# Storing the last of eight results through a SyncE register instead of a DMA

## Chip, cores, metric

One core of a Trainium2 chip. The metric is the device time of one execution in microseconds; a version is timed as the median of several executions. Times of this kernel agree within about 0.3 us from run to run.

## The reference

```python
# a, b: float32 [8, 2176, 2176]
prod = np.matmul(a, b)
return np.diagonal(prod, axis1=1, axis2=2).sum(axis=-1)     # 8 float32
```

Only the traces are wanted: each batch is the sum over the elements of `a` transposed times `b`. 303 MB of input give 32 bytes of output.

## The kernel before

All of `a` and `b` but the first 128 rows of `a` (1.1 MB, from SyncE's queue) is loaded from GpSimd's queue, which casts float32 to bfloat16 on the way. TensorE transposes `a`, ScalarE and VectorE copy the transposes from PSUM to SBUF ("evacuate"), VectorE multiplies and reduces (`multiply_reduce`), and in the last batch TensorE takes a part of the products into `trace_ps`. These parts matter here:

```python
def load(src, start, m):
    t = stage.tile([P, ROWS, N], bf16, tag="stage")
    rows = src[start:start + P * m, :].rearrange("(p r) k -> p r k", r=m)
    issued = nc.gpsimd.dma_start(out=t[:, 0:m, :], in_=rows)
    return t, issued
# ... the last row of b, in three pieces, also from GpSimd:
b_t = stage.tile([P, ROWS, N], bf16, tag="stage")
row = b_t[:, 0, :]
for g0, g1 in LAST_PIECES:                       # [(0, 2), (2, 3), (3, 5)]
    lo, hi = g0 * WIDE, min(g1 * WIDE, N)
    nc.gpsimd.dma_start(out=row[:, lo:hi], in_=b[bi, start:start + P, lo:hi])
# ...
multiply_reduce(tiles[f32], trace_ps, late_acc[:, len(late):len(late) + 1])

total = psum_small.tile([1, BATCH], f32, tag="total")
nc.tensor.matmul(
    total[:, 0:BATCH - 1], tiles["ones"], tiles["sums"][:, 0:BATCH - 1],
    start=True, stop=True,
)
parts = [tiles["sums"][:, BATCH - 1:BATCH]] + [late_acc[:, n:n + 1] for n in range(len(late) + 1)]
for n, part in enumerate(parts):
    nc.tensor.matmul(
        total[:, BATCH - 1:BATCH], tiles["ones"], part,
        start=(n == 0), stop=(n == len(parts) - 1),
    )
nc.vector.tensor_copy(out=tiles["result"][:1, :BATCH], in_=total)
nc.sync.dma_start(out=out.rearrange("(a b) -> a b", a=1), in_=tiles["result"][:1, :BATCH])
```

Behind this the build adds a closing sequence: each engine executes an instruction called DRAIN, SyncE checks the semaphores of all queues and engines one after the other (the "closing checks"), each engine signals to GpSimd at a barrier, GpSimd passes when all have signalled and releases them, and after a second round of that barrier the program ends. A transfer "lands" where the trace records the last semaphore update that it makes.

Of the kernel before, what the change touches and what calls it, by code (L numbers as in the profile page):

```python
# [20 lines left out]
def kernel(  # L21
# [6 lines left out]
    nc = tc.nc  # L28
    P = 128
    BATCH, N, N2 = a.shape  # L30
# [5 lines left out]
    f32 = mybir.dt.float32  # L36
# [9 lines left out]
    const = ctx.enter_context(tc.tile_pool(name="const", bufs=1))  # L46
# [5 lines left out]
    psum_small = ctx.enter_context(tc.tile_pool(name="psum_small", bufs=1, space=bass.MemoryType.PSUM))  # L52
# [18 lines left out]
    tiles = {}  # L71

    def constants():
        identity32 = const.tile([P, P], f32, tag="identity32")
        make_identity(nc, identity32)
        identity16 = const.tile([P, P], bf16, tag="identity16")
        make_identity(nc, identity16)
        ones = const.tile([P, 1], f32, tag="ones")
        nc.vector.memset(ones, 1.0)
        sums = const.tile([P, BATCH], f32, tag="sums")  # L80
        late = const.tile([P, 4], f32, tag="late")
        result = const.tile([P, BATCH], f32, tag="result")
        tiles.update(ones=ones, sums=sums, late=late, result=result)
        tiles[f32], tiles[bf16] = identity32, identity16

    evacs = 0
# [9 lines left out]
    def multiply_reduce(x, y, acc):  # L96
        scratch = scratch_pool.tile([P, N], bf16, tag="scratch")
        out = scratch[:, :math.prod(x.shape[1:])]
        if len(x.shape) == 3:
            out = out.rearrange("q (a b) -> q a b", b=x.shape[2])  # L100
        elif len(x.shape) == 4:
            out = out.rearrange("q (a b c) -> q a b c", b=x.shape[2], c=x.shape[3])
        nc.vector.tensor_tensor_reduce(  # L103
            out=out, in0=x, in1=y, scale=1.0, scalar=0.0,
            op0=MUL, op1=ADD, accum_out=acc,
        )
# [79 lines left out]
    late = []  # L186
    ahead = None
    for bi in range(BATCH):
# [6 lines left out]
        for start, m in order:  # L195
            if not tiles:
                a_t = load_first(a[bi], start)
                ahead, issued = load(a[bi], *order[1])
                with tc.issue_after(issued.ins):
                    constants()  # L200
            elif ahead is not None:
                a_t, ahead = ahead, None
            else:
                a_t, _ = load(a[bi], start, m)
            last_transpose = transpose_group(at, a_t, start, m, b_groups)
# [9 lines left out]
        for gi, (start, m) in enumerate(b_groups):  # L215
# [33 lines left out]
            out=tiles["sums"][:, bi:bi + 1], in_=acc[:, :cols], axis=mybir.AxisListType.X  # L249
# [4 lines left out]
    with tc.issue_after(last_transpose.ins):  # L254
        for n, (x, y) in enumerate(pe_work):
            nc.tensor.matmul(  # L256
                trace_ps, x, y, start=(n == 0), stop=(n == len(pe_work) - 1),
            )
    late_acc = tiles["late"]
    for n, (x, y) in enumerate(late):  # L260
        multiply_reduce(x, y, late_acc[:, n:n + 1])
    multiply_reduce(tiles[f32], trace_ps, late_acc[:, len(late):len(late) + 1])

    total = psum_small.tile([1, BATCH], f32, tag="total")
    nc.tensor.matmul(
        total[:, 0:BATCH - 1], tiles["ones"], tiles["sums"][:, 0:BATCH - 1],
        start=True, stop=True,
    )
    parts = [tiles["sums"][:, BATCH - 1:BATCH]] + [late_acc[:, n:n + 1] for n in range(len(late) + 1)]
    for n, part in enumerate(parts):  # L270
        nc.tensor.matmul(  # L271
            total[:, BATCH - 1:BATCH], tiles["ones"], part,
            start=(n == 0), stop=(n == len(parts) - 1),
        )
    nc.vector.tensor_copy(out=tiles["result"][:1, :BATCH], in_=total)
    nc.sync.dma_start(
        out=out.rearrange("(a b) -> a b", a=1),
        in_=tiles["result"][:1, :BATCH],
    )


# [28 lines left out]
```

## Time and profile before

| | before |
|---|---|
| time, median of the first 3 runs | 711.72 us (711.46 to 711.79) |
| span of the profiled execution | 709.78 us |
| last landing of `b` | 705.60 us |
| copy of the eight results ends on VectorE | 707.07 us |
| their store lands | 708.16 us |
| SyncE signals at the closing barrier | 708.31 us |
| GpSimd's closing drain ends | 709.03 us |
| GpSimd passes the barrier | 709.07 us |

Times inside a span count from its start; the last rows are read from the trace's records of semaphores and sequencers. The busy shares, the end of the timeline and the closing records are shown in the prediction below.

### The profile page before, as it was taken

The numbers are of one execution on the slowest core, as the hardware profiler recorded it, in microseconds if no ns is written. First come the engines' busy times: TensorE is split into PE (matmuls) and PEld (weight loads), VectorE is DVE, ScalarE is ACT, GpSimd is POOL, SyncE is SP. The second block draws the span as 40 slices with busy tenths as digits, with TensorE's granted clock in tenths as the row PEclk, the third lists the DMA queues.
The fourth block names the chain that finished last, engine by engine and source line by source line (L and its number), as shares of the span: only waits on it lengthen the run. The fifth ranks groups of instructions, "written<-read, shape, count | busy, mean of one in ns | idle before, by whom it ended". The sixth has DMA issues, their size and how long they took to land.

```text
span 709.8 us, 3800 instructions
## 1 busy us (share of the span) xinstructions
PE 233.3 (33%) x1406; PEld 221.8 (31%) x1406; DVE 408.9 (58%) x449; ACT 201.6 (28%) x210; POOL 45.2 (6%) x91
## 2 busy tenths in 40 slices
PE   2660025600345003540036400374003630036356
PEld 1660025600344003540036400374003630036355
DVE  0327972279812898219972199621996319963146
ACT  2651015600256002550035500354003630036300
POOL 2000000000000000000000000000000000000010
PEclk9866556755588555885556755666556875567755
DMA  9999999999999999999999999999999999999997
GB/s 220 220 220 219 206 219 219 220 218 206 221 219 218 218 210 218 220 218 214 213 219 219 218 213 214 220 218 216 213 217 219 218 216 212 218 218 216 219 210 139
DMA packets 12116, 152.32 MB, mean 215 GB/s; under 512 B 1346, under 2 KB 1602, under 8 KB 3778
## 3 DMA queue, kind: packets, MB, share of 16 engines
q0 software_dynamic: 11952, 150.97, 100.1%
q1 hardware_dynamic: 146, 1.11, 0.4%
q8 instruction: 11, 0.18, 0.1%
q14 instruction: 7, 0.06, 0.0%
HBM read 303.04 MB, written 0.00 MB: 427 GB/s over the span
## 4 chain that ended last, share of the span: by engine, by line
DMA 52%; issue 43%; POOL 3%; PE 2%; DVE 1%; another core or an unknown queue 0%; POOLq 0%; DVEq 0%
DMA t<-in_a_dram 42%; DMA t<-in_b_dram 6%; DMA b_t<-in_b_dram 3%; POOL t L57 2%; PE ps L136 1%; PE trace_ps L256 1%; DVE scratch L103 0%; DVE at L91 0%; POOL b_t L222 0%; POOLq L57 0%; PE ps L157 0%; POOL identity masks.py:199 0%; PE total L271 0%; POOL identity masks.py:197 0%
## 5 line engine op out<-in xcount | busy, mean ns | idle before, releaser
L103 DVE CUSTOM_DVE_ANT_1 scratch<-at,t 128x2048 bf16<-128x2048 bf16 (+1 forms) x156 | 310.5, 1990 | 85.5 <-DMA t<-in_b_dram 78.9
L136 PE MATMUL ps<-identity,t 128*128 128x128 f32 x1071 | 204.2, 372 | 460.3 <-DMA t<-in_a_dram 297.7
L136 PEld LDWEIGHTS ps<-identity,t 128*128 128x128 f32 x1071 | 193.7, 218 | 468.3 <-issue 302.8
L93 ACT COPY at<-ps 128x1024 bf16<-128x1024 bf16 x208 | 199.2, 1016 | 471.2 <-PE ps L136 471.1
L91 DVE COPY at<-ps 128x1024 bf16<-128x1024 bf16 (+2 forms) x104 | 92.8, 902 | 205.8 <-PE ps L136 198.9
L57 POOL DMA_DIRECT2D t<-in_a_dram x39 | 20.8, 535 | 329.5 <-DVE acc L103 230.2
L57 POOL DMA_DIRECT2D t<-in_b_dram x41 | 21.7, 530 | 304.2 <-PE ps L157 286.5
L256 PEld LDWEIGHTS <-at 128*128 128x128 bf16 x153 | 17.4, 124 | 12.0 <-issue 12.0
L256 PE MATMUL trace_ps<-t,at 128*128 128x128 bf16 x144 | 17.3, 294 | 10.2 <-DMA t<-in_b_dram 10.2
L157 PE MATMUL ps<-identity,t 128*128 128x128 bf16 x170 | 17.0, 224 | 2.2 <-DVE at L91 2.2
L157 PEld LDWEIGHTS <-t 128*128 128x128 bf16 x170 | 13.4, 102 | 3.8 <-issue 3.4
L103 DVE DVE_READ_ACCUMULATOR2_ANT acc<- 128x1 f32 x163 | 13.3, 82 | 0.0
L68 DVE CAST t<-words 128x1088 bf16<-128x1088 f32 x1 | 0.7, 726 | 4.9 <-DMA words<-in_a_dram 4.9
L103 DVE CUSTOM_DVE_ANT_0 scratch<-at,t 128x128 bf16<-128x128 bf16 x7 | 2.0, 291 | 0.2
L67 ACT CAST t<-words 128x1088 bf16<-128x1088 f32 x1 | 1.1, 1098 | 3.7 <-DMA words<-in_a_dram 3.7
L222 POOL DMA_DIRECT2D b_t<-in_b_dram x3 | 1.6, 539 | 3.6 <-PE trace_ps L256 3.6
L256 PE MATMUL trace_ps<-b_t,at 128*128 128x128 bf16 x9 | 1.5, 287 | 0.5 <-DMA b_t<-in_b_dram 0.4
L103 DVE CUSTOM_DVE_ANT_1 scratch<-at,b_t 128x256 bf16<-128x256 bf16 (+1 forms) x3 | 1.5, 510 | 0.2 <-DMA b_t<-in_b_dram 0.2
L248 DVE TENSOR_REDUCE sums<-acc 128x1 f32<-128x22 f32 (+1 forms) x8 | 1.4, 174 | 0.3
L67 ACT ACT_TABLE_LOAD x1 | 1.3, 1283 | 0.7 <-PEq L294 0.7
L271 PE MATMUL total<-late,ones 128*1 128x1 f32 x8 | 0.5, 163 | 0.3 <-DVE late L103 0.3
masks.py:199 POOL TENSOR_SCALAR_AFFINE_SELECT identity<-identity 128x128 f32<-128x128 f32 (+1 forms) x2 | 0.6, 308 | 0.0
(14 smaller groups left out, 2.4 us busy)
## 6 DMA issues: line engine op xcount, KB each, us to landing
t<-in_a_dram POOLq DMA_DIRECT2D x32, 2176.0 KB, 42.3
t<-in_b_dram POOLq DMA_DIRECT2D x31, 2176.0 KB, 47.2
t<-in_b_dram POOLq DMA_DIRECT2D x9, 544.0 KB, 39.5
t<-in_a_dram POOLq DMA_DIRECT2D x7, 544.0 KB, 35.0
words<-in_a_dram SPq DMA_DIRECT2D x1, 1088.0 KB, 5.0
t<-in_b_dram POOLq DMA_DIRECT2D x1, 1088.0 KB, 41.7
b_t<-in_b_dram POOLq DMA_DIRECT2D x1, 256.0 KB, 23.0
b_t<-in_b_dram POOLq DMA_DIRECT2D x1, 160.0 KB, 23.4
```

Of the source, the lines that this page charges most:

```text
L57: issued = nc.gpsimd.dma_start(out=t[:, 0:m, :], in_=rows)
L67: nc.scalar.copy(out=t[:, 0, :half], in_=plain[:, :half])
L68: nc.vector.tensor_copy(out=t[:, 0, half:], in_=plain[:, half:])
L91: nc.vector.tensor_copy(out=dst, in_=src)
L93: nc.scalar.copy(out=dst, in_=src)
L103: nc.vector.tensor_tensor_reduce(out=out, in0=x, in1=y, scale=1.0, scalar=0.0, op0=MUL, op1=ADD, accum_out=acc,)
L136: nc.tensor.transpose(ps[:, n * m + r, :], words[:, r, c0:c0 + step * (P - 1) + 1:step], tiles[f32],)
L157: last_transpose = nc.tensor.transpose(ps16[:, n, r, :], a_t[:, r, c0:c0 + P], tiles[bf16],)
L222: nc.gpsimd.dma_start(out=row[:, lo:hi], in_=b[bi, start:start + P, lo:hi])
L248: nc.vector.reduce_sum(out=tiles["sums"][:, bi:bi + 1], in_=acc[:, :cols], axis=mybir.AxisListType.X)
L256: nc.tensor.matmul(trace_ps, x, y, start=(n == 0), stop=(n == len(pe_work) - 1),)
L271: nc.tensor.matmul(total[:, BATCH - 1:BATCH], tiles["ones"], part, start=(n == 0), stop=(n == len(parts) - 1),)
```

## The change

Its intent: the store of the result at the very end is a DMA, which took 1.06 us from issue to landing. Seven of the eight results are known 74 us earlier, so they are stored then. For the eighth, SyncE loads the one word from SBUF into a register and stores it straight to memory, without a DMA.

```diff
+        last_sum = const.tile([P, 2], f32, tag="last_sum")
 ...
+    out_words = out.rearrange("(a b) -> a b", a=1)
+    result, last_sum = tiles["result"], tiles["last_sum"]
     total = psum_small.tile([1, BATCH], f32, tag="total")
     nc.tensor.matmul(
         total[:, 0:BATCH - 1], tiles["ones"], tiles["sums"][:, 0:BATCH - 1],
         start=True, stop=True,
     )
-    parts = [tiles["sums"][:, BATCH - 1:BATCH]] + [...]
+    nc.vector.tensor_copy(out=result[:1, :BATCH - 1], in_=total[:, :BATCH - 1])
+    nc.sync.dma_start(out=out_words[:, :BATCH - 1], in_=result[:1, :BATCH - 1])
+    final = psum_small.tile([1, 1], f32, tag="final")
+    parts = [tiles["sums"][:, BATCH - 1:BATCH]]
+    parts += [late_acc[:, n:n + 1] for n in range(len(late) + 1)]
     for n, part in enumerate(parts):
         nc.tensor.matmul(
-            total[:, BATCH - 1:BATCH], tiles["ones"], part,
-            start=(n == 0), stop=(n == len(parts) - 1),
+            final, tiles["ones"], part, start=(n == 0), stop=(n == len(parts) - 1),
         )
-    nc.vector.tensor_copy(out=tiles["result"][:1, :BATCH], in_=total)
-    nc.sync.dma_start(out=..., in_=tiles["result"][:1, :BATCH])
+    nc.vector.tensor_copy(out=last_sum[:1, 0:1], in_=final)
+    words = last_sum.bitcast(mybir.dt.int32)
+    last_word = out_words.bitcast(mybir.dt.int32)[:, BATCH - 1:BATCH]
+    word = nc.sync.alloc_register("word")
+    nc.sync.load(word, words[:1, 0:1])
+    nc.sync.store(last_word, word)
```

More of the change, by code (lines that the diff above doesn't have):

```diff
@@ L82, in constants @@
         result = const.tile([P, BATCH], f32, tag="result")
-        tiles.update(ones=ones, sums=sums, late=late, result=result)
+        last_sum = const.tile([P, 2], f32, tag="last_sum")
+        tiles.update(ones=ones, sums=sums, late=late, result=result, last_sum=last_sum)
         tiles[f32], tiles[bf16] = identity32, identity16
@@ L268 @@
     )
-    parts = [tiles["sums"][:, BATCH - 1:BATCH]] + [late_acc[:, n:n + 1] for n in range(len(late) + 1)]
+    nc.vector.tensor_copy(out=result[:1, :BATCH - 1], in_=total[:, :BATCH - 1])
[3 more added lines that the diff above has]
+    parts += [late_acc[:, n:n + 1] for n in range(len(late) + 1)]
     for n, part in enumerate(parts):
         nc.tensor.matmul(
-            total[:, BATCH - 1:BATCH], tiles["ones"], part,
-            start=(n == 0), stop=(n == len(parts) - 1),
-        )
-    nc.vector.tensor_copy(out=tiles["result"][:1, :BATCH], in_=total)
-    nc.sync.dma_start(
-        out=out.rearrange("(a b) -> a b", a=1),
-        in_=tiles["result"][:1, :BATCH],
-    )
+            final, tiles["ones"], part, start=(n == 0), stop=(n == len(parts) - 1),
+        )
+    nc.vector.tensor_copy(out=last_sum[:1, 0:1], in_=final)
[4 more added lines that the diff above has]
+    nc.sync.store(last_word, word)
 _INS = ['a', 'b']
```

## The prediction

> **What bounds the kernel now.** I began with the page: busy shares, slices, DMA queues.
>
> ```profile
> PE 233.3 (33%) x1406; PEld 221.8 (31%) x1406; DVE 408.9 (58%) x449; ACT 201.6 (28%) x210; POOL 45.2 (6%) x91
> DMA  9999999999999999999999999999999999999997
> q0 software_dynamic: 11952, 150.97, 100.1%
> ```
>
> No engine is over 58% busy, while the DMA engines are at nine tenths or more in 39 of 40 slices, and the queue fed by GpSimd alone takes 100.1% of the 16 engines' span. The kernel is a stream of `a` and `b` into SBUF; everything up to the last landing is set by that stream. The change touches nothing in it on purpose, so it can only act after the last landing, or by disturbing the stream. Next, the timeline of the last microseconds (start, duration, what).
>
> ```profile
> 705.64 0.50 PE L256 MATMUL trace_ps<-b_t,at 128*128 128x128 bf16 x3 [0.41 <-DMA b_t<-in_b_dram]
> 706.34 0.29 DVE L103 CUSTOM_DVE_ANT_0 scratch<-identity,trace_ps 128x128 bf16<-128x128 f32 x1 [0.18 <-PE total L271]
> 706.69 0.19 PE L271 MATMUL total<-late,ones 128*1 128x1 f32 x2 [0.28 <-DVE late L103]
> 706.91 0.15 DVE L275 COPY result<-total 1x8 f32<-1x8 f32 x1 [0.28 <-PE total L271]
> 707.10 0.32 SPq L276 DMA_DIRECT2D out_dram<-result  x1
> ```
>
> The last piece of `b` lands at 705.60 us, and 1.47 us of dependent work follow until the copy of the result ends at 707.07. SyncE issues the store at 707.10; the two semaphore updates of that DMA come at 707.54 and 708.16 us. The store costs 1.06 us from issue to landing. The span is 709.8 us, so 1.6 us come after even that. The chain of waits ends at the copy and says nothing of them; the sequencers' records of the line that closes the program do (count, then min/median/max ns, then first and last start).
>
> ```profile
> L305 SPq EVENT_SEMAPHORE  x8: 17/28/28, 707.5 to 709.7; - x8
> L305 POOLq EVENT_SEMAPHORE  x4: 17/17/17, 709.1 to 709.7; - x4
> L305 POOLq DRAIN  x3: 45/95/27027, 682.0 to 709.5; - x3
> L305 SPq DRAIN  x3: 7/7/7, 708.2 to 709.3; - x3
> ...
> SPq L305 <- PEq L305: 1.4, 2, 0.9
> SPq L305 <- DMA out_dram<-result: 0.4, 1, 0.4
> ```
>
> This is what decides the case. GpSimd begins its closing drain at 682.0 us, right behind its last load, and the drain lasts 27.027 us: it ends at 709.03. GpSimd then gathers the other engines at a barrier (709.07) and the program ends 0.71 us later. SyncE, which had the store to wait for (0.4 us of wait, the last line), reached that barrier at 708.31 us by the trace's semaphore record, and then waited 0.9 us. The view blames PE's sequencer for the 0.9, but PE had drained by 706.93: the one still missing was GpSimd. So the store of the result is *not* the last thing to arrive; it has 709.03 - 708.31 = 0.72 us of slack, if GpSimd's drain does not itself depend on that store.
>
> **What the Trainium skill says.** (1) "DMA: Bandwidth & Descriptors", section "Anatomy of one DMA", gives a DMA a fixed cost of about 2.0 us, most of it the write receipt. That is its fit for the GpSimd path; the trace here has 1.06 us for the 32-byte store from SyncE, so the prize is about half of what the page suggests. (2) The same page, "Latency and other measured facts", puts the floor of a `tensor_load` at about 600 ns. (3) "Runtime: NRT & Kernel Launch", section "Instruction fetch mechanics", puts a register load at about 200 ns a register in bulk and a store to HBM at about 73 ns, because a store is posted and a load is a round trip. The kernel before has neither, so its trace can't confirm (2) and (3). (4) The first page, "How a descriptor splits into AXI transactions": a descriptor that doesn't start on 256 B fetches from the boundary below. I use it for a side effect below.
>
> **The change part by part.** The order in which the built instructions stand shows where the scheduler put them.
>
> *Seven results early.* Their matmul already stands early (0.20 us at 632.74 us in the trace). Behind it DVE gets one copy of 1x7, about 0.15 us like the 1x8 copy. DVE is idle then: it ends an evacuation at 632.37 and has nothing until 633.65. Copy from about 632.96 to 633.12: hidden, with 0.5 us to spare. The 28-byte store runs from about 633.2 beside the stream: one or two small packets among 12116; the 32-byte one took 7 ns of one DMA engine. Cost 0.0 us, and its landing is 70 us before the end.
>
> *The arithmetic tail.* The same five final matmul pairs, now to a bank of their own, then a 1x1 copy in place of 1x8. 0.0 us; the copy again ends near 707.07.
>
> *The store.* Removed: the issue (0.32 us, 707.10 to 707.42) and its flight to 708.16. Added on SyncE, one behind the other: a load of the word from SBUF, a load of the output's 64-bit address from memory (two registers; the build adds it, the diff doesn't show it), one 64-bit addition, the store. Estimate from (2) and (3): 0.6 + 0.6 + 0.05 (sequencer steps at the end of this trace take 0.01 to 0.05) + 0.07 = 1.32 us. So the store is done at 707.10 + 1.32 = 708.42 us.
>
> *The closing waits.* Before, SyncE ran five of its six semaphore checks while the DMA flew: they start 0.06 us apart from 707.47 to 707.72, and only the sixth waited. Now all seven stand behind the store: a branch of 0.05, 7 x 0.062 = 0.43, and two drains of 0.055 each, 0.11. That is 0.59 us which used to lie beside the flight. SyncE reaches the barrier at 708.42 + 0.59 = 709.01 us, against 708.31 before: 0.70 us *later*.
>
> *The sum.* GpSimd ends its drain at 709.03 in either kernel. 709.01 against 709.03 is a tie: change 0.0 us if the loads cost their floor. The effect is one-sided: faster loads gain nothing because GpSimd is there, slower ones are paid in full. The skill's "about 1.3 us" for the load sequence of the launch (same runtime page) is an address read from HBM like the second load; with that in place of 0.6, SyncE arrives at 709.71 and the end moves by 0.68 us. I weigh the floor somewhat more than the other and take +0.2 us: 711.72 + 0.18 = 711.9 us.
>
> **The rivals.** *A: the store's latency was the end, and the register path saves it.* For it: SyncE waited on the store's landing, and GpSimd's drain ended 0.87 us after the landing, so it might be a consequence of it. Against it: GpSimd waits on no semaphore of that store, it was draining for 25 us before the store was issued, and its own last load landed at 705.60, 3.43 us before; a fixed overhead after that is as natural. If A holds and both loads take 0.2 us a register (three registers, 0.6 us in all), SyncE arrives at 708.3, as before: the gain is at most the drain's share, 0.7 us, so 711.0. I give a gain of over 0.3 us 12%.
>
> *B: two round trips cost much more than the floor.* Nothing in the trace speaks against it, since no register load is in it. At 1.3 us each the sum is 2.72, SyncE arrives at 710.41, and the time is 1.4 us longer: 713.1. I give over 0.9 us 10%.
>
> *C: the stream is disturbed.* The new tile of two words moves every large tile by 32 bytes in the build: the staging tiles started on multiples of 256 bytes and no longer do. 16 engines work all the time, so a slower packet would be paid 700 us long: 2% on each packet is 14 us, 726. For it: (4), if it holds for writes. Against it: a 17408-byte packet takes 1302 ns in every one of 8064 records, and it reads twice that, 34816 bytes of f32, for what it writes: 26.7 bytes per ns on the read side, 13.4 on the write side. One 256-byte step more on the side with half the load should hide. I give it 3%.
>
> **Range and chances.** The stream and the arithmetic are the same; the three times of before lie within 0.33 us, which is the noise. From below the range is held by GpSimd's drain (711.7 less noise, 711.3), from above by the uncertain price of two loads (712.7, where each load takes about 1.1 us instead of 0.6). Two per cent is 14.2 us, ten times all that the tail can hold; only C could reach it. Faster by over 2%: 1%; within: 97%; slower: 2%.
>
> **What would show it.** Right: GpSimd's drain ends again about 3.4 us after the last landing of `b`, whether or not a store flies; the SyncE store record ends at 708.4 or later; all the closing checks of SyncE come after it, 0.06 us apart; the seven-word store stands near 633 us; packets of 17408 bytes still take 1302 ns. Wrong: a drain that ends before 708.7 (then A, and the time falls below 711.3); register loads of over 1.1 us (B); packets longer than 1302 ns or a last landing after 706 us (C); or a DVE evacuation near 633.6 us that starts late.

## The result, and the profile after

711.97 us (711.82 to 712.18, 4 runs) against 711.69 us (711.46 to 711.79, 4 runs): 0.28 us longer. The ratio is 1.0005, 95% interval 0.9987 to 1.0022. Ratios here are the mean time of one kernel's fast runs over that of the other's of the same rounds, so not quite the ratio of the medians. The interval is wider than the effect; the executions of this series do not overlap, though, and a second series (run after_again below) gave nearly the same difference, 0.36 us.

The stream is what it was. From the page of the changed kernel:

```profile
DMA  9999999999999999999999999999999999999996
q0 software_dynamic: 11952, 150.97, 100.0%
```

The 8064 packets of 17408 bytes took 1302.30 ns on average, against 1302.31 before, so the shift of the tiles by 32 bytes changed nothing. The early part, in the timeline of the changed kernel (start, duration, what):

```profile
632.67 0.15 DVE L272 COPY result<-total 1x7 f32<-1x7 f32 x1 [0.61 <-PE total L268]
632.85 0.32 SPq L273 DMA_DIRECT2D out_dram<-result  x1
633.73 1.73 DVE L92 COPY at<-ps 128x1024 bf16<-128x1024 bf16 x2 [0.91 <-PE ps L137]
```

The extra copy fell into a hole of VectorE and ended 0.91 us before the next evacuation began, which waited for TensorE. Now the end: the timeline's last row, and then the records of the two source lines of the register path (count, min/median/max ns, first and last start).

```profile
707.01 0.15 DVE L283 COPY last_sum<-final 1x1 f32<-1x1 f32 x1 [0.28 <-PE final L280]
```

```profile
L287 SPq TENSOR_LOAD <-last_sum x1: 473/473/473, 707.2 to 707.2; - x1
```

```profile
L288 SPq TENSOR_LOAD <-out_dram_ptr x1: 1011/1011/1011, 707.7 to 707.7; - x1
L288 SPq ALU_OP  x1: 50/50/50, 708.8 to 708.8; - x1
L288 SPq TENSOR_STORE out_dram<- x1: 84/84/84, 708.8 to 708.8; - x1
```

Four steps stand one behind the other: the word, the output's address, the addition, the store. The store ends at 708.92 us, 1.74 us after the first load began at 707.18. The DMA before had landed 1.06 us after its issue. The records of the closing line, after the change:

```profile
L314 SPq EVENT_SEMAPHORE  x9: 20/28/31, 709.0 to 710.1; - x9
L314 POOLq EVENT_SEMAPHORE  x4: 17/17/17, 709.5 to 710.1; - x4
L314 POOLq DRAIN  x3: 45/102/27019, 682.1 to 709.9; - x3
L314 SPq DRAIN  x3: 13/13/15, 709.4 to 709.7; - x3
```

GpSimd's long drain, from 682.10 and 27.019 long, ends at 709.12, much as before (its last load also landed 0.09 us later). But SyncE's first closing check starts only at 709.0, and it signals at the barrier at 709.47, behind GpSimd. GpSimd passes at 709.495; its own drain would have let it pass at 709.118 + 0.044 = 709.162. The difference, 0.33 us, is the price of the change. The spans differ by 0.43: 0.09 from the landing of the stream, 0.33 from this wait, 0.01 behind it. SyncE's own waits after the change no longer hold a wait on a DMA, and the wait at the barrier has shrunk from 0.9 to 0.5 us:

```profile
SPq L287 <- DVE last_sum L283: 74.0, 1, 74.0
SPq L314 <- PEq L314: 0.6, 2, 0.5
```

### The profile page after: what moved, and what is told of

It is laid out like the page before. It is cut to its first block, busy times and chain, and to the rows that moved or that the text cites. A ratio compares the mean times of both kernels' runs of the same rounds, so it can differ in the third digit from the quotient of the medians.

```text
span 710.2 us, 3806 instructions
## 1 busy us (share of the span) xinstructions
PE 231.5 (33%) x1406; PEld 220.0 (31%) x1406; DVE 408.9 (58%) x450; ACT 201.2 (28%) x210; POOL 45.0 (6%) x91
## 4 chain that ended last, share of the span: by engine, by line
DMA 52%; issue 43%; POOL 3%; PE 2%; DVE 1%; another core or an unknown queue 0%; POOLq 0%; DVEq 0%
DMA t<-in_a_dram 42%; DMA t<-in_b_dram 6%; DMA b_t<-in_b_dram 3%; POOL t L57 2%; PE ps L137 1%; PE trace_ps L257 1%; DVE scratch L104 0%; DVE at L92 0%; POOL b_t L223 0%; POOLq L57 0%; PE ps L158 0%; POOL identity masks.py:199 0%; PE final L280 0%; POOL identity masks.py:197 0%
```

## The experiments

My theory had three parts. (1) GpSimd's closing drain sets the end in the kernel before, and it follows the last landing of GpSimd's own queue. (2) The store by DMA is hidden under it. (3) The register path is longer than the DMA, sticks out behind the drain, and whatever sticks out is paid in full. The main rival was that the way of the result to memory sets the end, and the drain only follows it.

One table for all traces, in us from the start of each span. "Signal" is the last signal at the closing barrier of any engine but GpSimd.

| kernel | last landing, GpSimd's queue | its drain ends | difference | signal | GpSimd passes | time (before, same rounds) |
|---|---|---|---|---|---|---|
| before | 705.595 | 709.027 | 3.432 | 708.306 | 709.071 | 711.69 |
| the change | 705.687 | 709.118 | 3.431 | 709.471 | 709.495 | 711.97 (711.69) |
| e1_no_last_word | 705.752 | 709.183 | 3.431 | 707.414 | 709.227 | 711.51 (711.54) |
| e2_word_loaded_twice | 705.671 | 709.102 | 3.431 | 709.896 | 709.919 | 712.35 (711.54) |
| e3_store_from_act | 705.812 | 709.243 | 3.431 | 709.371 | 709.394 | 711.69 (711.54) |
| e4_address_early | 705.796 | 709.227 | 3.431 | 708.605 | 709.271 | 711.53 (711.54) |
| after_again | 705.644 | 709.075 | 3.431 | 709.410 | 709.433 | 711.93 (711.57) |
| e5_last_row_by_sync | 702.899 | 706.207 | 3.308 | 709.355 | 709.378 | 711.48 (711.57) |
| e6_last_row_by_sync_address_early | 702.924 | 706.233 | 3.309 | 709.654 | 709.677 | 712.20 (711.57) |
| e7_last_row_by_sync_after | 702.977 | 706.285 | 3.308 | 710.533 | 710.557 | 712.77 (711.57) |
| e8_last_row_more_on_pe | 702.921 | 706.230 | 3.309 | 708.966 | 708.990 | 711.65 (711.55) |

GpSimd passes 0.044 us after its drain or 0.023 to 0.024 us after the last signal, whichever is later, in every row. The times in the last column are medians of all runs, while a trace is of one execution; that execution's own time is 2.47 to 2.55 us more than the moment at which GpSimd passes, in all eleven. So in these traces that moment sets the time.

### No last word at all

```diff
-    word = nc.sync.alloc_register("word")
-    nc.sync.load(word, words[:1, 0:1])
-    nc.sync.store(last_word, word)
```

> The changed kernel with the two lines that load and store the last word taken out; the eighth result is wrong on purpose. My theory (GpSimd's closing drain is the floor of the end): the drain ends again 3.43 us after the last landing of b, the end follows it by 0.75 us, and the time is that of the kernel before, 711.7 us, although SyncE reaches the barrier about 1.5 us before GpSimd. Rival (the path of the result to memory is what the end waits for, and the drain only follows it): with no such path the end comes 1.2 to 1.5 us earlier than before, 710.2 to 710.5 us.

711.51 us against 711.54 (ratio 1.000); the eighth result is missing. SyncE now waits for the last sum and for nothing behind it, and signals at 707.41 us, and the time is that of the kernel before. The records:

```profile
L311 POOLq DRAIN  x3: 45/95/27071, 682.1 to 709.7; - x3
L311 SPq DRAIN  x3: 7/7/7, 707.4 to 709.4; - x3
```

SyncE stands drained at 707.41 and is released only at 709.35, behind the drain of GpSimd (the 709.4 above is its drain in the second round). A free store would have gained nothing. This fells the main rival.

### The word loaded twice

```diff
+    again = nc.sync.alloc_register("again")
+    nc.sync.load(again, words[:1, 0:1])
     nc.sync.load(word, words[:1, 0:1])
+    nc.sync.reg_alu(word, word, again, mybir.AluOpType.bitwise_or)
     nc.sync.store(last_word, word)
```

> The changed kernel with the word loaded a second time into another register and the two joined by a bitwise or. My theory (SyncE arrived last at the closing barrier by 0.35 us, so all that is added to its chain is paid): one more load at 0.53 us start to start and one more register step of 0.08, 0.61 us more than the changed kernel: 712.6 us, 0.9 over before. Rival (the 0.3 us that the change lost are noise or a slower stream, and SyncE's chain is hidden): 712.0 us, as the changed kernel. Second rival (loads overlap one another): under 0.2 us more.

712.35 us, 0.81 over before. The changed kernel was 0.28 and 0.36 over before in its two series, so the second load cost 0.45 to 0.53. The sign and the mechanism are as expected, the size is smaller, because the second load is cheaper than the first:

```profile
L288 SPq TENSOR_LOAD <-last_sum x1: 472/472/472, 707.2 to 707.2; - x1
```

```profile
L289 SPq TENSOR_LOAD <-last_sum x1: 285/285/285, 707.7 to 707.7; - x1
```

From start to start the second load takes 0.34 us (707.694 to 708.036) and the extra register step 0.09, together 0.43, and in the traces GpSimd passes 0.42 us later than in the change (709.919 against 709.495): all of what is added is paid. The loads did not overlap.

### Load and store from ScalarE

```diff
-    word = nc.sync.alloc_register("word")
-    nc.sync.load(word, words[:1, 0:1])
-    nc.sync.store(last_word, word)
+    word = nc.scalar.alloc_register("word")
+    nc.scalar.load(word, words[:1, 0:1])
+    nc.scalar.store(last_word, word)
```

> The changed kernel with load and store of the last word on ScalarE, which has been idle since 677 us, instead of SyncE. My theory: the loads cost the same there, but SyncE's seven closing checks no longer stand behind the store, so the last engine but GpSimd reaches the barrier about 0.45 us earlier, at 709.0 us, just ahead of GpSimd's drain: 711.7 us, as before. Rival (it is the loads themselves that are exposed, the checks run beside them anyway): 712.0 us, as the changed kernel.

711.69 us, 0.15 over before (711.54 in these rounds), where I had expected none and the rival 0.3. SyncE, free of the store, signals at 708.04; its checks indeed left the chain. ScalarE's address load took 1042 ns, and its own drain behind the store took longer than I had reckoned:

```profile
L314 POOLq DRAIN  x3: 45/102/27018, 682.2 to 709.8; - x3
L314 ACTq DRAIN  x2: 8/128/249, 709.1 to 709.6; - x2
```

ScalarE's drain runs from 709.11 for 0.249 us, so ScalarE signals at 709.37, and GpSimd, whose drain ends at 709.24, still waits 0.11 us for it. Taking the checks out of the chain, less ScalarE's longer drain, is worth the 0.1 to 0.2 us gained on the changed kernel; the loads remain.

### The address loaded early

The build places the load of the output's address right before the store. Here it is written out by hand at 633 us, and the store uses the register pair.

```diff
+    address = nc.sync.alloc_register64("address")
+    nc.sync.load(address, nc.pointer_tensor(out.tensor).ap().bitcast(mybir.dt.int32))
+    nc.sync.reg_alu(address, address, 4 * (BATCH - 1), ADD)
 ...
-    nc.sync.store(last_word, word)
+    # one store instruction whose address operand is the pair `address`
```

> The changed kernel with the output's address loaded into registers and advanced by 28 bytes at about 633 us, right behind the early store, so that only the load of the word and the store stand behind the last sum. My theory: SyncE's chain is 1.1 us shorter and reaches the barrier at about 708.35 us, 0.75 us ahead of GpSimd's drain, so only the 0.3 us that the change had lost come back: 711.7 us. Rival (the register path sets the end and each us off it is a us off the time): 710.9 us, 0.8 under before.

711.53 us against 711.54. The early load took 1507 ns where nobody waits for it:

```profile
L267 SPq TENSOR_LOAD <-out_dram_ptr x1: 1507/1507/1507, 632.9 to 632.9; - x1
```

SyncE signals at 708.605, GpSimd passes at 709.271 after its own drain. A register path that is 0.97 us shorter (1.33 us from the end of the copy to SyncE's last drain, against 2.30) gives back only the 0.3 us that stuck out. Taking the address load out of the tail is enough to undo the loss; there is no gain beyond it.

### The change again, and one part of it alone

> The changed kernel unaltered, so that it has runs on the same chip and in the same rounds as the next three. All theories: 0.3 us over the kernel before, as on record (711.97 against 711.69).

711.93 us against 711.57. With the early store kept and the eighth result by a DMA of 4 bytes:

```diff
-    word = nc.sync.alloc_register("word")
-    nc.sync.load(word, words[:1, 0:1])
-    nc.sync.store(last_word, word)
+    nc.sync.dma_start(out=out_words[:, BATCH - 1:BATCH], in_=last_sum[:1, 0:1])
```

> One part of the change alone: seven results stored early, and the eighth by its own DMA of 4 bytes at the end instead of through a register. The tiles are shifted by 32 bytes as in the change. My theory: the early store, the extra copy and the shift cost nothing, and the DMA at the end is hidden under GpSimd's drain as in the kernel before: 711.55 us, as before, and all of the 0.35 us that the change loses belong to the register path. Rival (a part of the loss comes from the early store or the shift): between before and 711.9 us.

Four runs from 711.55 to 711.62, median 711.58 of those four, against 711.55: the early store and the shift of the tiles cost nothing, and the whole loss is the register path's. The fifth run, the profiled one, took 1023 us in a slow state in which TensorE's float32 transposes took 1046 ns instead of 372. Nothing of its time is used here, its cause stays open, and it is left out of the table. One relation can still be read in it: GpSimd's last load landed at 985.392 us, its drain ended at 988.824, again 3.432 us later, and the program went on for 32 us. The drain had not waited for the end of the program.

### GpSimd's drain taken out of the way

To see the two stores without the drain on top, the last row of `b` is loaded as float32 from SyncE's queue, held back until the row before the last but one has landed, and cast by ScalarE where TensorE needs bfloat16. GpSimd's last own load is then 2.7 us earlier.

```diff
-                row = b_t[:, 0, :]
-                for g0, g1 in LAST_PIECES:
-                    lo, hi = g0 * WIDE, min(g1 * WIDE, N)
-                    nc.gpsimd.dma_start(out=row[:, lo:hi], in_=b[bi, start:start + P, lo:hi])
+                plain = b_t.bitcast(f32).rearrange("p r k -> p (r k)")[:, :N]
+                row = b_t[:, 2, :]
+                nc.scalar.copy(out=plain[:1, 0:2049:512], in_=rows_of_b[-2][:1, 0, 0:5])   # holds the loads back
+                for lo, hi in LAST_PIECES:      # [(0, 1024), (1024, 1536), (2048, 2176), (1536, 2048)]
+                    nc.sync.dma_start(out=plain[:, lo:hi], in_=b[bi, start:start + P, lo:hi])
+                # ... nc.scalar.copy(out=row[...], in_=plain[...]) for TensorE's columns;
+                # VectorE multiplies straight from `plain`
```

> The kernel before with the last row of b loaded as float32 from SyncE's queue, held back until the row before the last but one has landed, and cast by ScalarE where TensorE needs it; store of the result as in the kernel before. GpSimd's last own load then lands before the end of the stream. My theory (the drain lasts until 3.43 us after the last landing of GpSimd's own queue): the drain ends at about 707.4 to 708.0 us instead of 709.0, while the last landing of the stream stays near 705.6; the result is ready some 0.3 us later for the cast, the store lands at 708.5 and now sets the end: about 711.1 us, 0.4 under before. Rival (the drain follows the last transfer of any queue): it ends at 709.0 or later and the time does not fall: 711.5 us or more.

711.48 us against 711.57: within the noise, not the 0.4 us under before that I expected. The part on the drain held in kind:

```profile
L320 POOLq DRAIN  x3: 45/101/29140, 677.1 to 709.8; - x3
L320 SPq DRAIN  x3: 7/7/7, 709.3 to 709.6; - x3
```

The drain runs from 677.07 for 29.140 us and ends at 706.21, although the stream's last piece, on SyncE's queue, landed only at 706.11 and the result's store at 709.21. So it follows GpSimd's own queue, whose last landing was at 702.90, and no other. It came earlier than the 707.4 to 708.0 that I had expected, and 3.31 us behind the landing instead of 3.43; what the 0.12 us are stays open. The end is now SyncE's. What ate the gain is the way to the result (the views show the type of one operand only; the second operand of the two products is float32):

```profile
705.92 0.61 DVE L103 CUSTOM_DVE_ANT_1 scratch<-at,b_t 128x256 bf16<-128x256 bf16 x1
706.13 0.42 ACT L232 CAST b_t<-b_t 128x256 bf16<-128x256 f32 x1 [0.16 <-DMA b_t<-in_b_dram]
706.58 0.61 DVE L103 CUSTOM_DVE_ANT_1 scratch<-at,b_t 128x256 bf16<-128x256 bf16 x1
707.96 0.15 DVE L290 COPY result<-total 1x8 f32<-1x8 f32 x1 [0.28 <-PE total L286]
```

The last landing came 0.5 us later than before, VectorE's products took 0.61 us with a float32 operand where they had taken 0.42, and the copy ended at 708.11, a whole microsecond later. The floor was gone, and the chain that it had covered had grown by more than the 0.74 us that it had in hand: GpSimd passes 0.31 us later than before. This trace is of the slowest of the five executions, 711.88 us; the others took 711.38, 711.38, 711.48 and 711.87. What parts them stays open, and even the fastest is only 0.19 us under before.

For the register path on the same ground, first with the early address, then as in the change:

> The same last row by SyncE, with the register path and the address loaded early. My theory: with GpSimd out of the way SyncE's chain sets the end; from the copy of the sum it took 1.34 us to the barrier in the run with the early address against about 1.2 us for the store by DMA in the kernel before, so this is 0.1 us slower than the last row with the DMA store: 711.2 us. Rival (drain follows any queue): 711.5 us, as the run with the early address alone.

> The same last row by SyncE, with the tail of the changed kernel as it is. My theory: here the full price of the register path shows, 2.2 us from copy to barrier against 1.2 us for the DMA store, because GpSimd's drain no longer covers 0.7 us of it: 1.0 to 1.1 us slower than the last row with the DMA store, 712.2 us. Rival (drain follows any queue): 0.3 us slower, as the change itself.

712.20 and 712.77 us: by the medians 0.72 and 1.29 us over the version with the DMA store, where I had expected 0.1 and 1.0 to 1.1. The first is a clear miss, also as a time (711.2 expected). But the medians do not compare like with like, as the runs of the DMA version lie in two groups. Between the traced executions it is 0.32 us (712.20 against 711.88) and 1.23 us (713.11 against 711.88), and the traces have 0.30 and 1.18 us of it at GpSimd's pass. The closing records of the second:

```profile
L329 POOLq DRAIN  x3: 45/108/29137, 677.1 to 711.0; - x3
L329 SPq DRAIN  x3: 13/13/15, 710.5 to 710.8; - x3
```

From the end of the copy to SyncE's last drain it took 2.41 us, against 1.23 with the DMA (708.109 to 710.517, and 708.113 to 709.346). So the register path is 1.2 us longer than the DMA here. In the change itself it is 1.07 us longer (2.30 against 1.23; it has two closing checks fewer), and GpSimd's drain hid all but 0.33 of that. With the early address the same stretch is 1.44 us, 0.21 more than the DMA, and the copy ended 0.08 us later in that trace: together nearly all of the 0.30. Its five runs spread over 0.8 us (711.90 to 712.72), and that spread stays open.

A second try at the last row, with three pieces, the products of the last two on TensorE alone and the last cast split between ScalarE and VectorE, and the store by DMA:

```diff
-                multiply_on_pe(...); late.append(...)     # VectorE's share of the last two pieces
+                cast(nc.scalar.copy, 3 * WIDE, split, 0, 2)
+                with tc.issue_after(before_casts.ins):
+                    cast(nc.vector.tensor_copy, 3 * WIDE, split, 2, ROWS)
+                    cast(nc.vector.tensor_copy, split, N, 0, ROWS)
+                multiply_on_pe(at, row, v0, 3, len(a_groups))
```

> The last row by SyncE with the result stored by DMA, once more, with the work behind the last landing cut: three pieces instead of four, the last two cast by ScalarE and VectorE and multiplied by TensorE alone, the last piece's cast split between the two. GpSimd's drain should end at about 706.2 us as in the first version, so the chain from the last landing to the store sets the end. That chain took 3.24 us to the barrier in the first version (706.11 to 709.35). My theory: VectorE's two products of 0.61 us leave it, a cast of 0.35 and some matmuls come in, the barrier is reached near 709.0 and the time is 711.1 to 711.2 us, 0.4 under before. Rival (something else, unseen, holds the end at 711.5): no gain.

711.65 us (711.49 to 712.11) against 711.55: no gain. The trace, of the fastest of the five executions, did what was foreseen (SyncE signals at 708.97), but I had set the time wrongly from it. Against the 709.07 at which GpSimd passes in the kernel before, that is 0.08 us, not 0.4. No version beats the kernel before by more than its noise; the kernel before stays the one to use.

## Why the prediction was right, point by point

- **What bounds the kernel, and who arrives last.** Right for the end, and shown by e1: without any last store the time does not move. That the drain keeps its distance from the last landing was argued in the prediction; in the seven fast traces with GpSimd's loads at the end it is 3.431 or 3.432 us.
- **Early store, arithmetic tail, shift of the tiles (rival C).** No cost, as said; shown by e9 and by the packets. One sign of being wrong seems to have come: VectorE's next evacuation began at 633.73 instead of 633.65 us. It had stood idle for 0.91 us and waited for TensorE, whose eight transposes took 1.76 us against 1.19; in the run after_again, with the same copy, they took 1.18 and the evacuation began at 633.28. So the copy did not hold it up.
- **The register path.** The steps and their order were right. The mis-sized term is the address load: 0.6 us taken, 1.04 us measured from its start to the next step. The word's load was 0.53 (0.6 taken), addition and store 0.20 (0.12). The sum is 1.78 us instead of 1.32, measured to the first closing check. Rival B's load of 1.3 us was too dear; the figure that the prediction takes from the runtime page is there for several registers' worth (a flag, addresses, pointers), and the address here is two registers.
- **The closing waits.** Estimated at 0.59, measured 0.52 us from the first check to SyncE's signal; e3 shows that they count only while nothing else is as late.
- **The sum.** A tie was found at the floor price, and +0.2 us was chosen between the two prices. 0.33 us stuck out in the trace and 0.28 to 0.36 in the times: the right side, near the middle of the two prices. The mechanism was derived, but the +0.2 was a weighing of two guesses at one load, and that it came so close is partly luck.
- **Rival A** had 12%. It fell with e1 and e5. Its arithmetic was a little off: with 0.6 us for the loads the prediction's own steps lead to 708.41, not 708.3.
- **A reading that was wrong.** The packets of 17408 bytes did not take 1302 ns in every record: 7989 of the 8064 took 1301 or 1302, the rest up to 1515, with a mean of 1302.31. The argument against rival C does not suffer from it.

## What to carry to other kernels

Before shortening the last step of a kernel, look at who arrives last at the closing barrier; here the longest record of the closing line, GpSimd's drain, was the last one and was not in the chain of waits at all. In this kernel, 3.3 to 3.4 us behind the last landing of GpSimd's queue were free for short work of other engines, until its drain ended; whether another kernel has the same is not shown here. A store through a register is not one step: word, address, addition and store stand behind each other, and the address can be loaded long before.

## What the Trainium skill lacked or had wrong

- GpSimd's closing drain behind its own loads is on no page. It ended 3.431 to 3.432 us after the last landing of its queue in the seven fast traces with GpSimd's loads to the end, and 3.308 or 3.309 us after it in the four in which the last row came from SyncE's queue. "VectorE: DVE Perf Modes", section "The DRAIN you can't avoid", speaks of drains of about 12 ns on all five engines, which it puts down to the runtime's sequences around a kernel; the one here stands in the program's own closing line, took 27 us and decided the end. What it does in the 3.4 us stays open.
- "DMA: Bandwidth & Descriptors", section "Latency and other measured facts": a `tensor_load` floor of about 600 ns. A word from SBUF took 456 to 475 ns, and 285 ns right behind another one.
- "Runtime: NRT & Kernel Launch", section "Instruction fetch mechanics": a bulk figure of about 200 ns a register for loads, and 73 ns for a store. The two-register address took 988 to 1042 ns after the end of the stream, 1111 and 1507 ns while it ran: about 500 ns a register at least. Stores took 71 to 93 ns, near what is stated, but 251 and 254 ns where the store followed the load of its word directly.
- "DMA: Bandwidth & Descriptors", section "Anatomy of one DMA": about 2.0 us fixed, fitted to the GpSimd path; the section has no such figure for SyncE's path. The 32-byte store from SyncE landed 1.06 us after its issue.
- The same page, "How a descriptor splits into AXI transactions", says what a start off 256 bytes costs a read. Writes into SBUF that were shifted by 32 bytes cost nothing measurable: 1302.30 ns a packet against 1302.31.
